# One softmax to a piece of other products, and gate chunks moved between the pairs of heads

## The chip, the cores and the metric

The kernel runs on one core of one Trainium2 chip. The metric is the device time of one execution in microseconds (us), less being better. TensorE multiplies, VectorE (DVE) and ScalarE (ACT) work on elements, GpSimd (POOL) does little here, and SyncE (SP) issues the loads. Each engine takes its instructions in one fixed order, and an instruction that must wait holds up all behind it on its engine.

## The reference

The work is a trunk of two layers over 256 latent tokens with 256 context tokens ahead of them, 2048 wide. Cut to what matters:

```python
for l in range(2):
    shift, scale, gate = silu(c) @ w_mod[l] + b_mod[l]      # 6144 numbers, also for c_ctx in layer 0
    h = rmsnorm(x) * (1 + scale) + shift
    q, k, v, g_att, u_pool, g_pool, a, b, g_conv = split(h @ w_in[l])   # 6656 columns
    s = q @ k.T / 8                        # 8 heads, two scores per head
    p = softmax(s)
    o = (p[0] - lam * p[1]) @ v
    y_att = rmsnorm(o) * silu(g_att)
    y_pool = pool(u_pool) * silu(g_pool)
    y_conv = conv(a, b) * silu(g_conv)     # depthwise, width 31, then a product of 512 by 512
    x = x + gate * (concat(y_att, y_pool, y_conv) @ w_out[l])
out = rmsnorm(x)                           # latent tokens only
```

Latent queries see all 512 keys; context queries see the 256 context keys only, and only in layer 0. In layer 1 the context goes no further than its keys and values.

## The kernel before

**Products.** Every large product is made of three products of numbers split in two: high by high, low by high, high by low. A weight piece of 128 by 1024 numbers (512 KB) is loaded by SP, copied to its high part by ScalarE (L205) and subtracted to its low part by VectorE (L206). The input projection is cut in 26 chunks of 256 columns, each four pieces of 24 matmuls; the output projection in eight chunks, o0 to o6 and "last". In layer 0, and in the k and v chunks of layer 1, a matmul of a chunk has 512 columns (FULL); in the other chunks of layer 1 it has 256 (HALF).

**What stands between the pieces.** The order of the chunks is written out by hand (`ORDER`, `ORDER_1`). The names are q, k, v, the gates ga (attention), gp (pooling), gc (convolution), the pooling input u and the convolution inputs a, b, with the number of the pair of heads or half. After each piece `project` calls `pump` (L251) with a budget, 3.4 for a FULL piece and 0.8 for a HALF one. `pump` takes steps from four queues in turn: `context_work`, `urgent` (attention and pooling), `conv_work`, `mod_work`. A step is a generator's run up to its next `yield`, and the number that it yields is taken off the budget. What the urgent queue leaves of a budget goes to the convolution, and what that leaves to `mod_work`. The recorded instructions are then put in order by a scheduler with priorities, engine by engine; the order that came out is shown below with the change.

**Attention.** `attention` (L709) works through the jobs of one pair of heads: per head two blocks of latent queries ("x") and in layer 0 the context ("c"). A job's front is its scores (`sx`, `sc`, L660) and its softmax (maximum L634 and the weighted difference L649 on VectorE, exponentials L640 on ScalarE, result `ex`). Its back is the transposes of `ex` (`atx`, L684), their split (`ahx`, `alx`) and the value products (`ox`, `oc`, L701 to L703). The front of job j is recorded before the back of the job ahead of it. A chunk q empties the urgent queue before it is taken, and so does a chunk ga whose pair has no normaliser yet.

**Modulation.** The 6144 numbers per layer that `c` gives are made in units of 1024 columns by `mod_on_dve` (L347) for the part that first-stage code does not cover: units (0,4), (0,5), then (1,0) to (1,3), and later (1,4), (1,5). A unit has 16 raws of 512 KB (`mraw`, loaded at L356 in two buffers) and for each raw two products on VectorE (one for `c`, one for `c_ctx`), added up in `macc` (L370, L372), of which there is one buffer. Then TensorE transposes `macc` (`modt`, L383), ScalarE adds up (L387) and `finish_mod` (L290, L293) writes the numbers. They are needed at the start of the next layer, and two places see to that: the queue gets what the budgets leave, and at o5 of each layer what is left of it is recorded at once:

```python
                ps = project(yh, yl, (0, L.n), f"o{i}_{l}")
                if i == 5:
                    drain(mod_work)
```

**The boundary of the layers.** Behind o6 the chunk "last" of layer 0 is multiplied in four parts (`ps_last`, 48 matmuls of 256 columns each). From its latent half the normaliser of layer 1 (`rms_v`, `rms_rstd`) and then `h` of layer 1 are made, on which `ps_b`, the first chunk of layer 1, depends.

Of the kernel before, what the change touches and what calls it, by code (L numbers as in the profile page):

```python
# [34 lines left out]


ORDER = (
    "b0 a0 q0 k0 v0 u0 b1 a1 q1 k1 v1 q2 k2 v2 q3 k3 v3 u1 ga1 gc0 ga2 gp0 ga0 ga3 gp1 gc1"
).split()
ORDER_1 = (  # L40
    "b0 a0 q0 k0 v0 u0 b1 a1 q1 ga0 k1 v1 q2 k2 gc1 v2 q3 k3 v3 u1 ga1 ga3 gc0 ga2 gp1 gp0"
).split()
OFFSET = {"q": 0, "k": 1024, "v": 2048, "ga": 3072, "u": 4096, "gp": 4608, "a": 5120, "b": 5632, "gc": 6144}

# [7 lines left out]
MOD_TAGS = ("whi", "wlo", "mraw", "whi", "wlo", "mraw", "whi", "wlo")  # L52

FULL, HALF = 3.4, 0.8
FRONT_0 = 2.0
FRONT, BACK = 1.5, 0.7
WAIT_MOD = 4.0
WAIT_CONV = 3.0

# [10 lines left out]
def trunk(  # L70
# [30 lines left out]
    def tmp(name, dt=F32):  # L101
        return tp.tile([P, T], dt, tag="t", name=name)
# [4 lines left out]
    def bank(name):  # L107
        return tr.tile([P, T], F32, tag="tr", name=name)
# [33 lines left out]
    def rsqrt(v, n, name, a=None, y=None):  # L142

        if a is None:
            nc.gpsimd.tensor_tensor(out=v, in0=v, in1=half[:, 0:1].to_broadcast([P, n]), op=ALU.pow)
            return
        nc.vector.tensor_scalar(
            out=y.bitcast(I32), in0=v.bitcast(I32), scalar1=-0.5, scalar2=1597463007.0, op0=ALU.mult, op1=ALU.add
        )
        for step in range(3):  # L150
            nc.vector.tensor_mul(out=a, in0=y, in1=y)
            nc.vector.scalar_tensor_tensor(out=a, in0=a, scalar=-0.5, in1=v, op0=ALU.mult, op1=ALU.mult)
            nc.vector.scalar_tensor_tensor(out=v if step == 2 else y, in0=a, scalar=1.5, in1=y, op0=ALU.add, op1=ALU.mult)
# [469 lines left out]
    def take_v(L, p, ps):  # L623
        L.vh = at.tile([P, 4, WC], F32R, tag="vh", name=f"vh{L.l}_{p}")
        L.vl = at.tile([P, 4, WC], F32R, tag="vl", name=f"vl{L.l}_{p}")
        with tc.high_priority(offset=V_BY):
            split_act(L.vh, L.vl, ps.rearrange("p b (c n) -> p (b c) n", n=WC))
        urgent.append(attention(L, p))
# [33 lines left out]
    def attend_front(L, p, h, which, qt):  # L662

        name = f"{which}{L.l}_{2 * p + h}_{qt}"
        ps = mm.tile([P, 2, T], F32, tag="mm", name=f"s{name}")
        if which == "x":
            scores(L, ps, slice(0, T), h, slice(qt * P, (qt + 1) * P), slice(0, T))
        else:
            for q in range(2):
                scores(L, ps, slice(q * TL, (q + 1) * TL), h, slice(TL + q * P, TL + (q + 1) * P), slice(TL, T))  # L670
        return softmax(L, ps, T, 1, name) if which == "x" else softmax(L, ps, TL, 2, name)

    def attend_back(L, p, h, which, qt, a):
        head = 2 * p + h
        name = f"{which}{L.l}_{head}"
        if qt == 0:
            L.ah = at.tile([P, 4, TL], F32R, tag="ah", name=f"ah{name}")
            L.al = at.tile([P, 4, TL], F32R, tag="al", name=f"al{name}")
        ah, al = L.ah, L.al
        b = bank(f"at{name}_{qt}")  # L680
        if which == "x":
            k0, nk, ts, qs = 0, 4, slice(0, TL), slice(qt * P, (qt + 1) * P)
            for kt in range(4):
                nc.tensor.transpose(b[:, kt * P : (kt + 1) * P], a[:, kt * P : (kt + 1) * P], ident)  # L684
            split_act(ah[:, :, qs], al[:, :, qs], b.rearrange("p (k q) -> p k q", q=P))
            if qt == 0:
                return
        else:
            k0, nk, ts = 2, 2, slice(TL, T)
            bv = b.rearrange("p (k q) -> p k q", q=TL)  # L690
            for q in range(2):
                for kt in range(2):
                    nc.tensor.transpose(
                        bv[:, kt, q * P : (q + 1) * P], a[:, q * TL + kt * P : q * TL + (kt + 1) * P], ident
                    )
            split_act(ah[:, :2, :], al[:, :2, :], bv)
        o = bank(f"o{name}")
        hs = slice(h * P, (h + 1) * P)
        for i in range(nk):
            kt = k0 + i  # L700
            nc.tensor.matmul(o[:, :TL], lhsT=L.vh[:, kt, hs], rhs=ah[:, i, :], start=i == 0, stop=False)  # L701
            nc.tensor.matmul(o[:, :TL], lhsT=L.vh[:, kt, hs], rhs=al[:, i, :], start=False, stop=False)
            nc.tensor.matmul(o[:, :TL], lhsT=L.vl[:, kt, hs], rhs=ah[:, i, :], start=False, stop=i == nk - 1)  # L703
        nc.scalar.copy(out=L.y[head][:, ts], in_=o[:, :TL])
        if which == "x":
            L.osq[h] = tmp(f"osq{name}")
        nc.scalar.activation(L.osq[h][:, ts], o[:, :TL], AF.Square)

    def attention(L, p):  # L709
        l, n = L.l, L.n  # L710
        L.osq = [None, None]
        jobs = []
        for h in range(2):
            jobs += [(h, "x", 0), (h, "x", 1)] + ([(h, "c", 0)] if L.ctx else [])
        prev = None
        for j in jobs:
            a = attend_front(L, p, *j)
            yield FRONT if prev else FRONT_0
            if prev:
                attend_back(L, p, *prev)  # L720
                yield BACK
            prev = j + (a,)
        attend_back(L, p, *prev)
        yield BACK

        nh = n // 2
        b = bank(f"ssq{l}_{p}")[:, :nh]
        for h in range(2):
            for half in range(2):
                c = 32 * (2 * h + half)  # L730
                nc.tensor.matmul(
                    b[c : c + 32, :], lhsT=ones[:, 0:32], rhs=L.osq[h][:, half * nh : (half + 1) * nh],
                    start=True, stop=True, skip_group_check=True,
                )
        v = one.tile([P, TL], F32, tag=f"arv{p}", name=f"arv{l}_{p}")[:, :nh]
        nc.vector.tensor_scalar(out=v, in0=b, scalar1=1.0 / P, scalar2=EPS, op0=ALU.mult, op1=ALU.add)
        work = tmp(f"arw{l}_{p}")
        rsqrt(v, nh, f"ars{l}_{p}", work[:, :nh], work[:, TL : TL + nh])
        L.arstd[p] = v
        yield 4.0  # L740
# [488 lines left out]
```

## Time and profile before

| what | value |
|---|---|
| median of 3 runs | 1495.96 us (1493.52 to 1496.93) |
| the profiled execution, its own time | 1502.84 us |
| its span, first to last instruction | 1501.0 us |
| TensorE busy | 1452.5 us (97%) |
| VectorE busy | 1112.8 us (74%) |
| ScalarE busy | 650.2 us (43%) |
| mean granted clock of TensorE | 0.992 |

The profiled execution lies 6.9 us above the median of the other runs, and 1.84 us of its time lie outside its span. Positions below are in us from the span's start. The stages, by the names of what TensorE writes: layer 0's attention chunks from 185 to 612, its other gates to 752, o0 to o5 to about 885, the boundary to 938, layer 1's attention from 1019 to 1365, the end 1501. A clock of 1.00 is TensorE's full granted speed, 2.4 GHz, and 0.5 the lower level of 1.2 GHz.

### The profile page before, as it was taken

Reading aid. Unit: us, or ns where it says so; the run is one execution under the profiler, and the core shown is the slowest. Engines: PE = TensorE matmul, PEld = TensorE weight load, DVE = VectorE, ACT = ScalarE, POOL = GpSimd, SP = SyncE. Lnnn points to the kernel's source line nnn. Section 1 sums busy time; section 2 is a strip of 40 time slices with the busy share of each in tenths; the row PEclk is TensorE's granted clock in tenths of the full one; section 3 lists DMA queues with packets and bytes.
Section 4 is the critical chain, followed back from the end, with each engine's and each line's share of the span. In section 5 each row is a group of like instructions: output and inputs, shape, how many; then the busy total and the mean of one; then the engine's idle time right before and its main releaser. Section 6 shows DMA issues by size and latency. Waiting matters only on the chain.

```text
span 1501.0 us, 23277 instructions
## 1 busy us (share of the span) xinstructions
PE 1452.5 (97%) x9196; PEld 1241.8 (83%) x9196; DVE 1112.8 (74%) x1641; ACT 650.2 (43%) x1245; POOL 9.0 (1%) x46
## 2 busy tenths in 40 slices
PE   4999999999999999999999999999999999999997
PEld 3567977897797977888888889988989897999997
DVE  4446999997549865879898964998995567475655
ACT  4224363227546363332433242635545545464543
POOL 0000000000000000000000000000000000000000
PEclk9999999999999999999999999999999999999998
DMA  8995226432234613655667761436733264245553
GB/s 332 397 391 221 81 88 202 148 110 74 74 112 146 202 60 113 221 195 203 209 213 250 243 222 55 142 114 216 265 113 124 79 227 161 99 134 178 187 183 113
DMA packets 75855, 258.90 MB, mean 172 GB/s; under 512 B 8800, under 2 KB 11104, under 8 KB 75744
## 3 DMA queue, kind: packets, MB, share of 16 engines
q1 hardware_dynamic: 75456, 257.14, 49.2%
q8 instruction: 72, 1.18, 0.3%
q14 instruction: 39, 0.32, 0.1%
q10 hardware_dynamic: 288, 0.26, 0.1%
HBM read 255.27 MB, written 2.10 MB: 171 GB/s over the span
## 4 chain that ended last, share of the span: by engine, by line
PE 83%; DVE 7%; DMA 4%; issue 3%; ACT 2%; SPq 0%; POOL 0%; POOLq 0%; DVEq 0%; ACTq 0%
PE ps_o L236 16%; PE ps_k L236 12%; PE ps_ga L236 9%; PE ps_v L227 7%; PE ps_q L236 6%; PE ps_gc L236 5%; PE ps_gp L236 4%; PE ps_first L236 4%; PE ps_b L236 3%; PE ps_u L236 3%; PE ps_a L236 3%; DMA mraw<-in_w_mod 3%; PE modacc L336 2%; DVE s L479 2%; DVE macc L372 1%
## 5 line engine op out<-in xcount | busy, mean ns | idle before, releaser
L372 DVE SCALAR_TENSOR_TENSOR macc<-mraw,c_sb,macc 128x1024 f32<-128x1024 f32 x210 | 262.6, 1280 | 32.2 <-DMA mraw<-in_w_mod 31.5
L236 PE MATMUL ps_o<-yh,out_h 128*128 128x512 f32 (+1 forms) x448 | 151.7, 339 | 0.0
L236 PE MATMUL ps_o<-yl,out_h 128*128 128x512 f32 (+1 forms) x448 | 151.6, 338 | 0.0
L236 PE MATMUL ps_o<-yh,out_l 128*128 128x512 f32 (+1 forms) x448 | 151.6, 338 | 0.0
L227 PE MATMUL ps_v<-in_v_h,hh 128*128 128x256 f32 x512 | 145.2, 284 | 0.0
L227 PE MATMUL ps_v<-in_v_h,hl 128*128 128x256 f32 x512 | 144.8, 283 | 0.0
L227 PE MATMUL ps_v<-in_v_l,hh 128*128 128x256 f32 x512 | 144.3, 282 | 0.0
L479 DVE SCALAR_TENSOR_TENSOR s<-cu,vec,s 128x512 f32<-128x512 f32 (+1 forms) x240 | 136.5, 615 | 0.5
L205 ACT CAST out_h<-out_r 128x1024 fp32r<-128x1024 f32 x56 | 58.8, 1050 | 111.5 <-PE ps_o L236 97.2
L236 PE MATMUL ps_k<-hh,in_k_h 128*128 128x512 f32 x256 | 102.9, 402 | 1.9 <-ACT ex L640 1.0
L236 PE MATMUL ps_k<-hl,in_k_h 128*128 128x512 f32 x256 | 102.1, 399 | 0.0
L236 PE MATMUL ps_k<-hh,in_k_l 128*128 128x512 f32 x256 | 101.8, 398 | 0.0
L227 PEld LDWEIGHTS ps_v<-in_v_l,hh 128*128 128x128 f32 x512 | 96.7, 189 | 0.3
L227 PEld LDWEIGHTS ps_v<-in_v_h,hh 128*128 128x128 f32 x512 | 96.7, 189 | 0.3
L227 PEld LDWEIGHTS ps_v<-in_v_h,hl 128*128 128x128 f32 x512 | 96.4, 188 | 0.0
L236 PEld LDWEIGHTS ps_o<-yl,out_h 128*128 128x128 f32 x448 | 84.3, 188 | 9.9
L236 PEld LDWEIGHTS ps_o<-yh,out_h 128*128 128x128 f32 x448 | 84.3, 188 | 9.9
L236 PEld LDWEIGHTS ps_o<-yh,out_l 128*128 128x128 f32 x448 | 84.3, 188 | 9.8
L206 DVE TENSOR_TENSOR out_l<-out_r,out_h 128x1024 fp32r<-128x1024 f32 x56 | 68.1, 1223 | 32.1 <-ACT out_h L205 30.7
L236 PE MATMUL ps_ga<-hh,in_ga_h 128*128 128x512 f32 (+1 forms) x256 | 87.2, 340 | 1.0 <-ACT ex L640 1.0
L236 PE MATMUL ps_ga<-hl,in_ga_h 128*128 128x512 f32 (+1 forms) x256 | 87.0, 340 | 0.0
L236 PE MATMUL ps_ga<-hh,in_ga_l 128*128 128x512 f32 (+1 forms) x256 | 87.0, 340 | 0.0
(407 smaller groups left out, 3708.2 us busy)
## 6 DMA issues: line engine op xcount, KB each, us to landing
mraw<-in_w_mod SPq DMA_DIRECT2D x128, 512.0 KB, 4.3
wm<-in_w_mod SPq DMA_DIRECT2D x64, 512.0 KB, 8.5
out_r<-in_w_out SPq DMA_DIRECT2D x56, 512.0 KB, 4.0
in_k_r<-in_w_in SPq DMA_DIRECT2D x32, 512.0 KB, 4.4
in_v_r<-in_w_in SPq DMA_DIRECT2D x32, 512.0 KB, 3.4
in_ga_r<-in_w_in SPq DMA_DIRECT2D x32, 512.0 KB, 3.8
in_q_r<-in_w_in SPq DMA_DIRECT2D x28, 512.0 KB, 3.5
in_u_r<-in_w_in SPq DMA_DIRECT2D x16, 512.0 KB, 3.4
```

Source lines behind the costliest of these rows:

```text
L205: nc.scalar.copy(out=hi, in_=raw)
L206: nc.vector.tensor_sub(out=lo, in0=raw, in1=hi.bitcast(F32))
L227: nc.tensor.matmul(o, lhsT=a[:, ts], rhs=b[:, j, :], start=f and n == 0 and tt % 2 == 0, stop=e and n == 2, skip_group_check=True,)
L236: nc.tensor.matmul(ps[:, nt, t0:t1], lhsT=a[:, j, ns], rhs=b[:, t0:t1], start=f and n == 0, stop=e and n == 2,)
L336: nc.tensor.matmul(acc[c : c + 32, :n], lhsT=sc32[:, k, :], rhs=raw[:, j, :], start=k < 4, stop=k >= KT - 4, skip_group_check=True,)
L372: nc.vector.scalar_tensor_tensor(out=acc[:, r, :], in0=raw, scalar=sc[:, k, r : r + 1], in1=acc[:, r, :], op0=ALU.mult, op1=ALU.add)
L479: nc.vector.scalar_tensor_tensor(out=acc, in0=u[:, :nq, j : j + TL], scalar=w[:, j : j + 1], in1=acc, op0=ALU.mult, op1=ALU.add)
```

## The change

Three things are changed. First, `attention` yields once per job and no longer twice: the front of job j, then the back of the job ahead of it, then one yield of 3.4 (layer 0) or 2.4 (layer 1). So a FULL piece's budget of 3.4 takes one whole job in layer 0, where before it took a front of 1.5, a back of 0.7 and the next front. For a pair with six jobs in layer 0 that is seven steps that each use up a budget (six jobs and the last back with what follows), against four budgets before. Second, in `ORDER` ga0 and ga1 move up, from the end of the layer to between the pairs. Third, in `ORDER_1` ga0 moves from inside pair 1 to behind v1, gp0 from the end to behind it, and ga1 from behind u1 to between pair 2's and pair 3's chunks.

```diff
--- before.py
+++ after.py
@@ -35,10 +35,10 @@
 
 
 ORDER = (
-    "b0 a0 q0 k0 v0 u0 b1 a1 q1 k1 v1 q2 k2 v2 q3 k3 v3 u1 ga1 gc0 ga2 gp0 ga0 ga3 gp1 gc1"
+    "b0 a0 q0 k0 v0 u0 b1 a1 q1 k1 v1 ga0 q2 k2 v2 ga1 q3 k3 v3 u1 gc0 ga2 gp0 ga3 gp1 gc1"
 ).split()
 ORDER_1 = (
-    "b0 a0 q0 k0 v0 u0 b1 a1 q1 ga0 k1 v1 q2 k2 gc1 v2 q3 k3 v3 u1 ga1 ga3 gc0 ga2 gp1 gp0"
+    "b0 a0 q0 k0 v0 u0 b1 a1 q1 k1 v1 ga0 gp0 q2 k2 v2 gc1 ga1 q3 k3 v3 u1 ga2 gc0 ga3 gp1"
 ).split()
 OFFSET = {"q": 0, "k": 1024, "v": 2048, "ga": 3072, "u": 4096, "gp": 4608, "a": 5120, "b": 5632, "gc": 6144}
 
@@ -52,8 +52,7 @@
 MOD_TAGS = ("whi", "wlo", "mraw", "whi", "wlo", "mraw", "whi", "wlo")
 
 FULL, HALF = 3.4, 0.8
-FRONT_0 = 2.0
-FRONT, BACK = 1.5, 0.7
+ATTEND, BACK = (3.4, 2.4), 0.7
 WAIT_MOD = 4.0
 WAIT_CONV = 3.0
 
@@ -715,10 +714,9 @@
         prev = None
         for j in jobs:
             a = attend_front(L, p, *j)
-            yield FRONT if prev else FRONT_0
             if prev:
                 attend_back(L, p, *prev)
-                yield BACK
+            yield ATTEND[l]
             prev = j + (a,)
         attend_back(L, p, *prev)
         yield BACK
```

Three places show how the instructions move. The names in a row are output<-inputs, with the scheduler's buffer numbers at the end; the number before them is the line.

**VectorE at the boundary of the layers.** The unit in question is unit 3 of layer 1 (`macc1_3`, raws `mraw1_3_0` to `_15`). Before, from `out0_6_0_l` on, VectorE has only splits of weights and residuals `s` here:

```order
L206 TENSOR_TENSOR out0_6_0_l_7621<-out0_6_0_r_7618,out0_6_0_h_7620 128x1024
L290 TENSOR_TENSOR mod1_119<-modsum1_3_7545,vec1_85 128x16
L293 SCALAR_TENSOR_TENSOR mod1_119<-mod1_119,vec1_85 128x16
L206 TENSOR_TENSOR last0_0_1ql_7794<-last0_0_r_7791,last0_0_0qh_7793 128x1024
L206 TENSOR_TENSOR out0_6_1_l_7666<-out0_6_1_r_7663,out0_6_1_h_7665 128x1024
L206 TENSOR_TENSOR last0_1_1kl_7800<-last0_1_r_7797,last0_1_0kh_7799 128x1024
L807 SCALAR_TENSOR_TENSOR s10_y_3676<-ps_o5_0_7482,mod0_118,xr5_0_7478 128x256 x2
L807 SCALAR_TENSOR_TENSOR s11_y_3677<-ps_o5_0_7482,mod0_118,xr5_1_7479 128x256 x2
L206 TENSOR_TENSOR out0_6_3_l_7696<-out0_6_3_r_7693,out0_6_3_h_7695 128x1024
L1075 TENSOR_TENSOR sq_acc_120<-sq_acc_120,nsq0_10_7650 128x512
L206 TENSOR_TENSOR last0_3_1vl_7806<-last0_3_r_7803,last0_3_0vh_7805 128x1024
L1075 TENSOR_TENSOR sq_acc_120<-sq_acc_120,nsq0_11_7655 128x512
```

Of the change, the rows from the eleventh raw of unit 3 on (line numbers are one or two lower than before):

```order
L371 SCALAR_TENSOR_TENSOR macc1_3_7514<-mraw1_3_10_7579,c_sb_83,macc1_3_7514 128x1024 x2
L371 SCALAR_TENSOR_TENSOR macc1_3_7514<-mraw1_3_11_7583,c_sb_83,macc1_3_7514 128x1024 x2
L205 TENSOR_TENSOR last0_1_1kl_7800<-last0_1_r_7797,last0_1_0kh_7799 128x1024
L371 SCALAR_TENSOR_TENSOR macc1_3_7514<-mraw1_3_12_7587,c_sb_83,macc1_3_7514 128x1024 x2
L371 SCALAR_TENSOR_TENSOR macc1_3_7514<-mraw1_3_13_7591,c_sb_83,macc1_3_7514 128x1024 x2
L805 SCALAR_TENSOR_TENSOR s12_103<-ps_o6_0_7662,mod0_118,xr6_0_7658 128x256 x2
L805 SCALAR_TENSOR_TENSOR s13_104<-ps_o6_0_7662,mod0_118,xr6_1_7659 128x256
L371 SCALAR_TENSOR_TENSOR macc1_3_7514<-mraw1_3_14_7595,c_sb_83,macc1_3_7514 128x1024 x2
L371 SCALAR_TENSOR_TENSOR macc1_3_7514<-mraw1_3_15_7599,c_sb_83,macc1_3_7514 128x1024 x2
L805 SCALAR_TENSOR_TENSOR s13_104<-ps_o6_0_7662,mod0_118,xr6_1_7659 128x256
L205 TENSOR_TENSOR last0_3_1vl_7806<-last0_3_r_7803,last0_3_0vh_7805 128x1024
L205 TENSOR_TENSOR last0_2_1al_7812<-last0_2_r_7809,last0_2_0ah_7811 128x1024
```

All 32 products of unit 3 now stand between `out0_6_0_l` and `last0_3_1vl`, with the splits of out0_6_1, out0_6_3, out0_6_2 and last0_1 among them and those of last0_3 and last0_2 behind the last product. Before, the last of these products stood ahead of `out0_5_3_l`. What came before in the layer is shifted by a unit: `macc1_0` starts behind the split of in0_ga3 where it started behind that of in0_ga2.

**TensorE at unit 3's transposes.** Before, `modt1_3` stands within o5:

```order
L236 MATMUL ps_o5_0_7482<-yh0_7_6619,out0_5_1_l_7486 128x512
L383 MATMUL modt1_3_0_7546<-ident_82,macc1_3_7109 128x128 x4
L383 MATMUL modt1_3_2_7556<-ident_82,macc1_3_7109 128x128 x4
L236 MATMUL ps_o5_0_7482<-yh0_12_6623,out0_5_3_h_7517 128x512
L236 MATMUL ps_o5_0_7482<-yl0_12_6624,out0_5_3_h_7517 128x512
L236 MATMUL ps_o5_0_7482<-yh0_12_6623,out0_5_3_l_7518 128x512
L236 MATMUL ps_o5_0_7482<-yh0_12_6623,out0_5_3_h_7517 128x512
L236 MATMUL ps_o5_0_7482<-yl0_12_6624,out0_5_3_h_7517 128x512
L383 MATMUL modt1_3_4_7566<-ident_82,macc1_3_7109 128x128 x4
```

Of the change it stands within the first half of "last":

```order
L235 MATMUL ps_last0_0_1_7864<-yh0_12_6516,last0_3_0vh_7805 128x256
L235 MATMUL ps_last0_0_1_7864<-yl0_12_6517,last0_3_0vh_7805 128x256
L382 MATMUL modt1_3_0_7606<-ident_82,macc1_3_7514 128x128
L382 MATMUL modt1_3_2_7616<-ident_82,macc1_3_7514 128x128
L382 MATMUL modt1_3_0_7606<-ident_82,macc1_3_7514 128x128 x3
L382 MATMUL modt1_3_2_7616<-ident_82,macc1_3_7514 128x128 x3
L235 MATMUL ps_last0_1_0_7937<-yh0_0_6478,last0_0_0qh_7793 128x256
L235 MATMUL ps_last0_1_0_7937<-yl0_0_6479,last0_0_0qh_7793 128x256
L235 MATMUL ps_last0_0_0_7815<-yh0_12_6516,last0_3_1vl_7806 128x256
L382 MATMUL modt1_3_4_7626<-ident_82,macc1_3_7514 128x128 x4
```

So `modt1_3`, which needs the last product into `macc1_3`, moved from o5 to the middle of "last". Where `modt1_3` stood in o5 there is now `modt1_2`. Between the end of `modt1_2` and the first row of `modt1_3` TensorE has 137 matmuls of o5 and o6 and 52 of "last"; 140 of the 192 of "last" stand behind it.

**TensorE at the first softmaxes of layer 0.** Before, `sx0_0_0` and `sx0_0_1` stand side by side, then come the 24 matmuls of a piece of u0, and then:

```order
L236 MATMUL ps_u0_0_1788<-hh0_7_135,in0_u0_1_l_1792 128x512
L660 MATMUL sc0_0_0_1894<-kh0_0_1528,qh0_0_1362 128x256 x2
L660 MATMUL sc0_0_0_1894<-kl0_0_1529,qh0_0_1362 128x256 x2
L660 MATMUL sc0_0_0_1894<-kh0_0_1528,ql0_0_1363 128x256 x2
L660 MATMUL sc0_0_0_1894<-kh0_0_1528,qh0_0_1362 128x256 x2
L684 MATMUL atx0_0_0_1887<-ident_82,ex0_0_0_1828 128x128 x4
L660 MATMUL sc0_0_0_1894<-kl0_0_1529,qh0_0_1362 128x256 x2
L660 MATMUL sc0_0_0_1894<-kh0_0_1528,ql0_0_1363 128x256 x2
L660 MATMUL sx0_1_0_1945<-kh0_0_1528,qh0_0_1362 128x512 x2
```

Of the change, a piece of u0 stands between `sx0_0_0` and `sx0_0_1`, and the transposes come two matmuls behind the latter:

```order
L235 MATMUL ps_u0_0_1788<-hh0_7_135,in0_u0_1_l_1792 128x512
L659 MATMUL sx0_0_1_1867<-kh0_0_1528,qh0_0_1362 128x512 x2
L659 MATMUL sx0_0_1_1867<-kl0_0_1529,qh0_0_1362 128x512 x2
L659 MATMUL sx0_0_1_1867<-kh0_0_1528,ql0_0_1363 128x512 x2
L235 MATMUL ps_u0_0_1788<-hh0_12_145,in0_u0_3_h_1839 128x512
L235 MATMUL ps_u0_0_1788<-hl0_12_146,in0_u0_3_h_1839 128x512
L683 MATMUL atx0_0_0_1887<-ident_82,ex0_0_0_1828 128x128 x4
L235 MATMUL ps_u0_0_1788<-hh0_12_145,in0_u0_3_l_1840 128x512
L235 MATMUL ps_u0_0_1788<-hh0_12_145,in0_u0_3_h_1839 128x512
```

From the end of `sx0_0_0` to `atx0_0_0` TensorE now has 24 matmuls of u0, three rows of scores and two matmuls of u0; before it had the three rows of `sx0_0_1`, the 24 matmuls and four rows of `sc0_0_0`.

## Rows read from the trace of the kernel before

**Rows 1.** The page, first part: engine, busy us, share of the span, instructions.
```profile
PE 1452.5 (97%) x9196; PEld 1241.8 (83%) x9196; DVE 1112.8 (74%) x1641; ACT 650.2 (43%) x1245; POOL 9.0 (1%) x46
```

**Rows 2.** Busy time by stage (--windows), all engines, with granted clock.
```profile
752.00:877.00 125.00, 125.00 (x545) 100.70 (x544) 113.11 (x119) 35.92 (x69) 0.00 (x0) 1.00 0.71 238
877.00:938.00 61.00, 60.55 (x371) 53.41 (x370) 27.94 (x48) 22.38 (x57) 1.16 (x7) 1.00 0.34 115
```

**Rows 3.** The same view, TensorE alone, first part of the boundary of the layers.
```profile
877.00:912.60 35.60, 35.60 (x162) 1.00 0.53 181
```

**Rows 4.** The same view, instructions that touch macc alone, on two stretches.
```profile
752.00:877.00 125.00, 2.35 (x16) 1.92 (x17) 71.15 (x58) 1.00 0.71 238
877.00:938.00 61.00, 2.35 (x16) 1.63 (x15) 0.00 (x0) 1.00 0.34 115
```

**Rows 5.** Chain of waits at the boundary: start, length, what.
```profile
877.21 0.87 PE modt L383 x8
...
880.88 31.84 PE ps_o L236 x137
...
912.75 1.23 DVE s L807 x3
...
926.23 0.70 POOL rms_v L145
...
926.98 0.71 PE rms_rstd L160 x4
927.69 9.84 PE ps_last L236 x83
937.53 7.47 PE ps_b L236 x63
```

**Rows 6.** VectorE's timeline before and at the boundary: start, length, what.
```profile
858.15 4.86 DVE L372 SCALAR_TENSOR_TENSOR macc<-mraw,c_sb,macc 128x1024 f32<-128x1024 f32 x4
...
882.26 0.17 DVE L290 TENSOR_TENSOR mod<-modsum,vec 128x16 f32<-128x16 f32 x1 [2.90 <-ACT modj L387]
```

**Rows 7.** Source view of L356 (the loads of raws), 800 to 880 us.
```profile
L356 SPq DMA_DIRECT2D mraw<-in_w_mod x18: 327/328/328, 800.7 to 872.6; - x18
...
DMA to landing us min/median/max: 3.4/4.4/4.7
```

**Rows 8.** Waits of TensorE in layer 0's attention: us, times, longest.
```profile
PE atx L684 <- DVE ex L649: 2.3, 3, 1.6
PE oc L701 <- ACT ahc L212: 1.1, 2, 0.6
...
PE ox L701 <- DVE alx L213: 0.7, 1, 0.7
```

**Rows 9.** A lone softmax of layer 1 on VectorE's timeline.
```profile
1307.08 1.23 DVE L206 TENSOR_TENSOR in_u_l<-in_u_r,in_u_h 128x1024 fp32r<-128x1024 f32 x1 [0.41 <-ACT in_u_h L205]
...
1312.51 0.75 DVE L649 SCALAR_TENSOR_TENSOR ex<-ex,rx 128x512 f32<-128x512 f32 x1
```

**Rows 10.** TensorE's timeline, the end of the scores of that softmax.
```profile
1306.89 0.39 PE L236 MATMUL ps_u<-hh,in_u_h 128*128 128x256 f32 x1
```

**Rows 11.** Waits of TensorE in layer 1's attention.
```profile
PE atx L684 <- DVE ex L649: 6.2, 2, 3.6
PE ps_k L236 <- ACT ex L640: 1.0, 1, 1.0
PE ps_ga L236 <- ACT ex L640: 1.0, 1, 1.0
```

**Rows 12.** Busy time and granted clock around the two longest of these waits.
```profile
1030.00:1039.00 9.00, 6.44 (x39) 5.69 (x39) 8.76 (x14) 5.55 (x12) 0.00 (x0) 0.81 0.70 221
...
1247.00:1250.80 3.80, 3.80 (x15) 2.05 (x13) 3.09 (x5) 3.53 (x8) 0.00 (x0) 0.52 0.60 215
1250.80:1258.20 7.40, 7.40 (x35) 6.34 (x35) 6.32 (x9) 3.24 (x9) 0.00 (x0) 0.79 0.53 155
```

**Rows 13.** VectorE's timeline, a product that waits for its raw in layer 1.
```profile
1231.69 1.28 DVE L372 SCALAR_TENSOR_TENSOR macc<-mraw,c_sb,macc 128x1024 f32<-128x1024 f32 x1 [0.94 <-DMA mraw<-in_w_mod]
```

## The prediction

> **What bounds the kernel now.** I read the page's first part, then the busy time by stage, and only then the waits, because the share of TensorE says where anything can be won at all. TensorE is busy for 1452.5 us of a span of 1501.0, VectorE for 1112.8 [rows 1], so the kernel is a queue of matmuls, and a change of order can only win what TensorE now waits, or lose by making it wait. At the output projection there is nothing to win: from 752 to 877 TensorE is busy all the time, while VectorE works 113.1 of 125 us [rows 2], 71.2 of them on the products into `macc` [rows 4]. At the boundary of the layers, 877 to 938, VectorE has only 27.9 us of work in 61 [rows 2] and none of it is `macc` [rows 4], since the last unit of layer 1's numbers was finished in o5; TensorE runs without a gap from 877 to 912.6 [rows 3], and behind it the chain goes on through "last" to `ps_b`, the first chunk of layer 1, at 937.53 [rows 5]. So there is slack on VectorE in one place, and the change puts something into it.
>
> **What can be won.** In layer 0's attention TensorE waits 2.3 us for `ex`, 1.1 for `ahc` and 0.7 for `alx`, 4.1 in all [rows 8]. In layer 1's attention it waits 6.2 us for `ex` in two waits and twice 1.0 for the exponentials, 8.2 in all [rows 11]. Behind a long wait the granted clock falls: 0.52 for 3.8 us and 0.79 for 7.4 us after the wait of 3.6, 0.81 in the stretch of 9 us with the wait of 2.6 [rows 12]. A clock of 0.5 is the lower of the two levels, so 0.52 means 3.6 us at the lower level, 0.79 some 3.1 us and 0.81 some 3.4 us; half of each is lost: 1.8 + 1.55 + 1.7 = 5.1 us. All that the change could win is therefore 4.1 + 8.2 + 5.1 = 17.4 us.
>
> **Term 1, the boundary.** A pair of layer 0 takes seven budgets where it took four, so less reaches `mod_work`, and the units of layer 1's numbers run late. The order shows by how much: unit 2's transposes stand where unit 3's stood in o5, and all 32 products of unit 3 come behind them. There is one `macc` buffer, so the first product waits for the end of unit 2's transposes, which I put where unit 3's end now, at 880.88 [rows 5].
>
> The work of VectorE from there to the last product: four products take 4.86 [rows 6], 1.2 each; 30 at 1.2 and the first two of a unit, which are plain products, at some 0.7 (an estimate) make 37.5. Among them stand five splits of weights (last0_0, out0_6_1, out0_6_3, out0_6_2, last0_1) at 1.15 (the 1.23 of [rows 9] less the overlap of neighbours), 5.7; seven residuals at 1.23/3 = 0.41 [rows 5], 2.9; and `finish_mod`, two of 0.17 [rows 6], 0.3. Sum 46.4: with every raw there in time the last product would end at 927.3.
>
> The raws are not there in time. A load is issued when its buffer is free, that is after the second product of the raw two before it, and lands a median 4.4 us later (3.4 to 4.7) [rows 7]. Two products take 2.4. A raw thus comes round every 6.8 us in each of two buffers, and two raws are used per round: 882.4 (first raw done) + 7 x 6.8 + 2.4 = 932.4. The splits and residuals lie inside the waits. I take 932.4, the later of the two limits.
>
> TensorE's work until it needs the last product: 137 matmuls take 31.84 [rows 5], then 52 of 256 columns at 9.84/83 = 0.119 [rows 5], 6.2. Together 38.0: it is done at 918.9 and waits 13.5 us for `modt1_3`, in one piece or partly ahead of o6's late splits. Two splits of "last" stand behind the last product, so it goes on at about 934. Then come 0.9 for the transposes [rows 5], 140 matmuls at 0.12, 16.8, and some 1.7 for the chain of the normaliser (0.70 and 0.71 in [rows 5], and a residual); `ps_b` starts at about 953.4 instead of 937.5, **+16**. A wait of this length has a lower clock behind it; the like of rows 12 would be 1.5 to 3.4 us, but the wait may come in several pieces. I add 1: **+17**. Bounds: with landings hidden +11 with the clock, with 4.7 instead of 4.4 seven rounds add 2.1, with the full price of the clock 2.4 more, +22.
>
> The Trainium skill ("Trainium Kernel Development and Optimization", Best Practices) says that double buffering overlaps loads with compute. By that rule the two buffers of raws hide the loads and the boundary costs +11 in place of +17; the trace disagrees so far, since a landing of 4.4 [rows 7] is longer than the 2.4 of products that cover it, and VectorE waits 0.94 for such a raw in layer 1 [rows 13].
>
> **Term 2, layer 0's attention.** The distance between a softmax's scores and its transposes hardly changes: 24 x 0.232 + scores 0.85 + two matmuls 0.5 = 7.0 us. A lone softmax in layer 1 takes from 1306.89, when its scores are done [rows 10], to 1313.25, 6.4 us with one split in its way [rows 9]. So it fits by 0.6, and the back-to-back scores that now make VectorE do two maxima in a row are gone. A product into `macc` (1.2) on top would cost 0.6. Some of the waits should go: I take -2.5, between -4.1 (all) and +5 (some eight softmaxes of the last pair with 0.6 each, because `macc` now stands densely there).
>
> **Term 3, layer 1's attention.** The order of pair 0 is the same, so its wait of 2.6 stays. Pair 2's backs move from a chunk of k (pieces of 24 x 0.232 = 5.6 us) under ga1 (24 x 0.119 = 2.9). There VectorE has four splits (4.8), five products into `macc` (6.0) with waits for raws of some 0.8 (an estimate by the 0.94 of [rows 13]), 4, and some 10.9 of softmax and gate work, 25.7, while TensorE has 20.3: up to +5.4 new. The other pairs have 19 of VectorE under 24 of TensorE. Against that stand the second wait of 3.6 and the two of 1.0, which may go. I take +1.5, between -13.3 (all waits and the clock) and +7.
>
> The gates' moves cost nothing by themselves: the same matmuls, splits and loads, hidden under TensorE as before; if the cover is gone it is what term 3 says. Loads on SP move with their chunks; raws of unit 3 stand among those of "last" and of layer 1's first chunk, which by the sum are needed later than they land.
>
> **Sum.** 17 - 2.5 + 1.5 = +16 on the span of 1501.0: 1517. The profiled execution took 1502.84, 1.84 beyond its span, and lies 6.9 above the median of the runs, 1495.96; I carry the +16 over to the median: **1512**.
>
> **The rivals.**
>
> *A: the waits of the attention go, and that outweighs the boundary.* For it: scores are now spread out, one maximum at a time, and most waits are for `ex`. With all 17.4 won and +11 to +17 lost at the boundary the time is 1489.5 to 1496; it decides as soon as the boundary costs less than the attention wins. Against it: pair 0 of layer 1 keeps its order, and with it 2.6 us and its 1.7 of clock, so 13.1 are the most that I see. Chance 0.14, split into 0.09 faster and 0.05 the same; time 1494.
>
> *B: the double buffer hides the raws.* Then the boundary is bound by VectorE's 46.4 us: +11, and the sum is +10, 1506. For it: the shortest landing of 3.4, and the splits and residuals among the products, which give the loads more time. Against it: the median of 4.4. Chance 0.22.
>
> *C: ga1 and the pairs of layer 1 become bound by VectorE, and the loads of raws land late.* +7 in place of +1.5 and +22 in place of +17: +26.5, 1522. For it: waits for raws in layer 1 [rows 13]. Against it: mean work of VectorE stays below TensorE's. Chance 0.12.
>
> The Trainium skill ("TensorE: Matmul & The Clock Gate", HAM oscillation) says that gaps in TensorE's work bring the clock down, so one gap costs more than its length. The traces agree at 0.52 behind the 3.6 us [rows 12]; by it the boundary could cost up to 2.4 more than I take.
>
> **How the numbers follow.** My forecast, +13 to +20, has 0.52. The range of eight in ten leaves out rival A and the far half of C: **1500 to 1521**. About 0.2% (3 us) is what a measurement of this kernel can tell from no change. Faster by more than that 0.09 (A), within it 0.07 (A's rest and the low end of B), slower 0.84.
>
> **What would show it.** Right: in 880 to 950 of the changed profile TensorE idles 8 to 15 us with `macc` or a raw as the releaser, VectorE's `macc` work there is about 38 us where it was none, the raws' landing is the releaser of `macc` in every round, `ps_b` of layer 1 starts about 13 to 16 us later than before, a lower clock shows behind the gap; up to o5 the time lies 2 to 3 us ahead of before. Rival B: `macc` runs without gaps. Rival A: no wait for `ex` left in either layer. The prediction is wrong if TensorE's idle time at the boundary is under 5 us, for instance because loads land faster there or because o6's splits come in time, or if a wait in the attention grows instead of shrinking.

## The result

The changed kernel takes 1513.78 us (median, 1510.26 to 1514.44, 4 runs) against 1496.45 of the kernel before beside it (1493.52 to 1498.2, 4 runs). The ratio is 1.0113, with a 95% interval of 1.0094 to 1.0133, so 14 to 20 us slower. The forecast was 1512.

**The profile after.** The page's first part of the changed kernel, as in [rows 1]:

```profile
PE 1457.2 (96%) x9196; PEld 1241.4 (82%) x9196; DVE 1115.5 (74%) x1641; ACT 662.8 (44%) x1253; POOL 8.9 (1%) x46
```

The span is 1512.2 us. VectorE's work is the same within 3 us, and TensorE's within 5, so it is not more work but work at another place. Busy time by stage (all engines, then granted clock, share of the DMA engines and GB/s), the stretches that answer to [rows 2]; the boundary now ends at 953, not at 938:

```profile
752.00:877.00 125.00, 125.00 (x550) 101.01 (x548) 111.78 (x116) 36.04 (x77) 0.00 (x0) 1.00 0.71 236
877.00:953.00 76.00, 65.11 (x380) 56.88 (x380) 65.50 (x84) 24.88 (x83) 1.17 (x7) 0.93 0.59 198
```

The same view for the instructions that touch `macc`, answering to [rows 4]:

```profile
752.00:877.00 125.00, 3.38 (x24) 2.72 (x24) 70.92 (x58) 1.00 0.71 236
877.00:953.00 76.00, 5.71 (x24) 3.79 (x24) 38.30 (x32) 0.93 0.59 198
```

Up to 877 nothing has changed: 70.9 us of VectorE on `macc` where there were 71.2, and TensorE busy all the time. Behind it stand 32 products, 38.3 us, where there were none. The chain of waits at the boundary (start, length, what), answering to [rows 5]:

```profile
750.33 55.77 PE ps_o L235 x240
...
878.20 0.57 PE modt L382 x4
...
886.33 4.73 DMA mraw<-in_w_mod
...
902.37 4.32 DMA mraw<-in_w_mod
...
920.12 4.19 DMA mraw<-in_w_mod
...
927.99 1.29 DVE macc L371
929.33 1.54 PE modt L382 x6
...
951.77 8.90 PE ps_b L235 x75
```

The reader is to see that the chain, which before ran along TensorE's own rows, now runs from a raw's transfer (three steps of 4.2 to 4.7 us are shown) to products into `macc`, to the last product at 927.99 to 929.3, and over the transposes of unit 3 back to TensorE. `ps_b` of layer 1 starts at 951.77 instead of 937.53 [rows 5], though o0 starts 1.9 us earlier, at 750.33.

The chain's steps through loads are longer than what the loads cost, because VectorE does splits and residuals while a raw is under way. VectorE alone from unit 3's first product to its last, and then from the source view of the loads (L355, 870 to 930 us) who waited for them and how long they took to land:

```profile
878.80:929.28 50.48, 46.66 (x47) 0.96 0.68 226
...
  DVE macc L371: 3.5, 5
...
DMA to landing us min/median/max: 3.3/3.9/4.7
```

It works 46.7 of the 50.5 us and idles 3.5 for raws, five times. TensorE's waits at the boundary (us in all, times, longest):

```profile
PE modt L382 <- DVE macc L371: 8.8, 2, 8.3
PE ps_last L235 <- DVE last_1kl L205: 0.9, 1, 0.9
PE ps_o L235 <- DVE out_l L205: 0.7, 1, 0.7
PE ps_last L235 <- DVE s_y L805: 0.5, 1, 0.5
```

and its clock (busy us, granted clock, share of the DMA engines, GB/s):

```profile
929.00:933.00 4.00, 3.67 (x16) 0.50 0.69 229
933.00:937.00 4.00, 4.00 (x29) 0.75 0.86 303
...
1260.00:1264.00 4.00, 4.00 (x15) 0.50 0.78 221
1264.00:1268.00 4.00, 4.00 (x28) 0.74 0.38 134
```

Behind the wait of 8.3 the clock is 0.50 for 4 us and 0.75 for the next 4, that is 2 + 1 = 3 us lost; the last two rows are the same fall in layer 1, behind a wait of 3.0. The waits of the attention, layer 0 as [rows 8] and then layer 1 as [rows 11]:

```profile
PE atx L683 <- DVE ex L648: 2.7, 1, 2.7
PE ox L701 <- DVE alx L212: 0.9, 5, 0.2
...
PE oc L700 <- ACT ahc L211: 0.4, 2, 0.2
```

```profile
PE atx L683 <- DVE ex L648: 6.0, 3, 3.0
```

In layer 0 the sum is what it was, 4.0 for 4.1, but 2.7 of it are now in one wait, where the longest was 1.6 [rows 8]. Behind that wait the clock falls, which it does nowhere in layer 0's attention before (busy us, granted clock, share of the DMA engines, GB/s):

```profile
583.00:587.00 4.00, 4.00 (x14) 0.57 0.69 218
```

That is 1.7 us lost. In layer 1 the waits are 6.0 for 8.2, in three waits instead of four.

### The profile page after: what moved, and what is told of

Read it like the earlier page. It is cut to its first block, busy times and chain, and to the rows that moved or that the text cites. A ratio compares the mean times of both kernels' runs of the same rounds, so it can differ in the third digit from the quotient of the medians.

```text
span 1512.2 us, 23250 instructions
## 1 busy us (share of the span) xinstructions
PE 1457.2 (96%) x9196; PEld 1241.4 (82%) x9196; DVE 1115.5 (74%) x1641; ACT 662.8 (44%) x1253; POOL 8.9 (1%) x46
## 4 chain that ended last, share of the span: by engine, by line
PE 82%; DVE 7%; DMA 6%; ACT 3%; issue 2%; SPq 0%; POOL 0%; DVEq 0%; POOLq 0%; ACTq 0%
PE ps_o L235 13%; PE ps_k L235 11%; PE ps_ga L235 9%; PE ps_v L226 8%; PE ps_q L235 7%; PE ps_first L235 4%; DMA mraw<-in_w_mod 4%; PE ps_gp L235 4%; PE ps_gc L235 4%; DVE macc L371 3%; PE ps_u L235 3%; PE ps_b L235 3%; PE ps_a L235 3%; PE modacc L335 2%; PE sx L659 1%
```

## The experiments

Two changes of the kernel, yields and chunk orders, act on two layers, so I undid them one at a time, then took the late unit itself away. For the comparison I read three lengths off TensorE's timeline in each run: from the first matmul of k0 to the first of o0 in layer 0, from there to layer 1's first chunk (the boundary with the output projection ahead of it), and from there to layer 1's o0. Single executions, in us, good to about 0.1; the medians of the kernel before in the four batches are 1496.4 to 1497.4, and each ratio is to its own batch:

| kernel | median | ratio to before, interval | k0 to o0 | o0 to layer 1 | layer 1 to its o0 |
|---|---|---|---|---|---|
| before | 1496.45 | | 612.2 | 185.4 | 460.7 |
| the change | 1513.78 | 1.0113 [1.0094, 1.0133] | 611.6 | 201.4 | 458.9 |
| e1, old yields | 1503.32 | 1.0038 [1.0025, 1.0051] | 614.6 | 185.5 | 459.1 |
| e2, old orders | 1511.33 | 1.0083 [1.0058, 1.0107] | 619.2 | 193.4 | 454.9 |
| e3, layer 1's part alone | 1500.03 | 1.0012 [0.9999, 1.0025] | 612.1 | 185.4 | 460.5 |
| e4, layer 0's part alone | 1511.04 | 1.0084 [1.0061, 1.0108] | 609.7 | 201.8 | 453.4 |
| e5, e4 with budget 4.6 | 1513.47 | 1.0104 [1.0084, 1.0123] | 618.2 | 196.1 | 455.7 |
| e6, e4 with budget 5.8 | 1534.63 | 1.0251 [1.0228, 1.0274] | 641.9 | 194.6 | 453.5 |
| e7, unit 3 cut to two raws | 1501.71 | 1.0032 [1.0018, 1.0046] | 612.3 | 188.4 | 458.9 |
| e8, three buffers of raws | 1525.3 (one run) | | 608.4 | 213.3 | 460.8 |
| e9, e5 with three buffers | 1503.7 | 1.0041 [1.0025, 1.0057] | 599.8 | 205.4 | 456.7 |
| e10, before with three buffers | 1496.0 | 0.9992 [0.9977, 1.0007] | 611.5 | 185.5 | 454.1 |
| e11, layer 1's yields alone | 1496.52 | 0.9993 [0.9979, 1.0007] | 612.0 | 185.4 | 453.7 |

In e9 the scheduler set the first matmuls of o0 among the last gate chunk, so there only the sum of two columns means something: 805.2, against 814.3 in e5, 836.5 in e6, 797.6 before and 811.5 in e4. The last column also shows that layer 1 of the kernel before, in the execution whose rows were shown, was 4 to 7 us longer than the same order and yields of layer 1 in e4, e5, e6, e9 and e10 (453.4 to 456.7). That is where most of that execution's 6.9 us above the median lay.

**e1, the new chunk orders with the old yields.** Edit against the changed kernel (the constants are left out):

```diff
-            if prev:
-                attend_back(L, p, *prev)
-            yield ATTEND[l]
+            yield FRONT if prev else FRONT_0
+            if prev:
+                attend_back(L, p, *prev)
+                yield BACK
```

> The changed chunk orders with the yields of before (front and back apart). In its order unit 3 of layer 1's numbers ends in o5 again, as before the change. Theory (the late unit at the boundary of the layers costs 16 us and the rest next to nothing): 1494 to 1499, no macc at the boundary and TensorE busy there. Rival (the gates between the pairs, that is the chunk orders, make the loss): 1508 to 1514 with new waits in the attention.

1503.32, between the two theories: the boundary is back at 185.5, 16 us shorter than in the change, so the late unit makes that part. But layer 0 is 3 us longer than in the change, and 6 us above the kernel before remain. TensorE waits in layer 0 up to o0:

```profile
PE atx L684 <- DVE ex L649: 5.0, 4, 2.0
```

5.0 us for `ex`, where before it was 2.3 [rows 8], and layer 1 takes 459.1 instead of 454. By these single executions the chunk orders with gates between the pairs cost some 2.4 in layer 0 and 5 in layer 1 by themselves.

**e2, the new yields with the old orders.** Edit against the kernel before:

```diff
-            yield FRONT if prev else FRONT_0
             if prev:
                 attend_back(L, p, *prev)
-                yield BACK
+            yield ATTEND[l]
```

> The new yield (one softmax to a piece) with the chunk orders of before. In its order unit 3 starts in o4's last piece and ends within the boundary, some 28 us earlier than in the changed kernel. Theory (late unit): the last product is done about 28 us earlier, by about 905, before TensorE needs it, so the boundary costs 0 to 3 and the time is 1495 to 1500. Rival (the new yields themselves lose in the attention): 1508 to 1514.

1511.33, a miss for the theory and within the rival's range. The first half of it: in layer 0 the new yields with the old orders lose 7 us. Waits that were not there (up to o0):

```profile
PE ps_k L235 <- ACT ex L639: 3.4, 2, 1.7
PE atx L683 <- DVE ex L648: 1.9, 1, 1.9
PE oc L701 <- DVE alc L212: 1.9, 2, 0.9
```

All waits there are 8.1 us where they were 5.2, so they alone are not the 7. Twice a wait of 0.9 and one of 1.7 stand close together, and there the granted clock is low (TensorE's busy us, clock, share of the DMA engines, GB/s):

```profile
372.00:379.00 7.00, 5.93 (x18) 0.52 0.01 2
474.00:481.50 7.50, 5.82 (x22) 0.55 0.00 0
```

That is 3.4 us lost each time, 6.7 in all, while some 2 us of transposes are gone from here to the boundary: most of the 7 is the clock. The second half is the boundary. Unit 3 did start earlier, but the chain shows that it was slower than I took it:

```profile
855.78 0.57 PE modt L382 x4
...
895.01 3.87 DMA last_r<-in_w_out
...
907.82 3.77 DVE macc L371 x3
```

It starts at the end of unit 2's transposes, 856.4, some 22 us earlier than in the change and not 28, and ends at 911.6, 55 us later where the change takes 50: among the products stand splits and residuals, and once one that waits for a weight's landing (895.01, 3.87). `modt` stands earlier on TensorE too, in o6, and waits there (2.3 us), and the boundary is 8 us longer than before. The rival is right for 7 us, the late unit for 8.

**e3 and e4, each layer's part alone.** e3 has the change's `ORDER_1` and yield 2.4 in layer 1 alone, e4 its `ORDER` and yield 3.4 in layer 0 alone; the edit is the diff above with a condition on `l`:

```diff
-            yield FRONT if prev else FRONT_0
+            if l == 0:
+                yield FRONT if prev else FRONT_0
...
+            if l == 1:
+                yield ATTEND
```

> Layer 0 as before, layer 1's order and yields of the change. Theory (late unit, which is layer 0's doing): 1493 to 1498, boundary as before at about 937. Rival (layer 1's chunks of 256 columns become bound by VectorE): 1503 to 1512, waits in layer 1 longer than the 6.0 us of the change.

> Layer 0's order and yields of the change, layer 1 as before; the late unit is as in the change. Theory (late unit): all of the loss, 1511 to 1516, ps_b of layer 1 starts at about 952. Rival (layer 1 makes half of the loss or more): 1500 to 1505.

e4 keeps the late unit and all but 3 us of the loss (1511.04), with a boundary of 201.8. e3 takes 1500.03, 2.7 above its own kernel before: between the theories, and the interval (0.9999 to 1.0025) does not exclude no change. It is about what e4 lacks to the whole (2.7 between the medians, 3.6 when each is held against its own batch). In the third length, single executions, layer 1 takes 460.5 where the old order takes 453.4 to 456.7 in all but one.

**e11, layer 1's yields without its order.** Against the kernel before; the old yields are kept for layer 0:

```diff
+            if l == 1:
+                yield ATTEND
```

> The kernel before with layer 1's yield of the change alone (2.4 once per softmax), all chunk orders as before. Theory (layer 1's loss of some 3 us comes from the gates between its pairs, whose pieces of 2.9 us stand where pieces of 5.6 stood): 1494 to 1498, no loss. Rival (the yield makes it): 1499 to 1502, as with the whole of layer 1's part.

1496.52, no loss, so the yields of layer 1 cost nothing that can be measured. The loss goes with the order: all five runs with the new `ORDER_1` take 458.9 to 460.8 in the last column, seven of the eight with the old one 453.4 to 456.7 (the eighth is the kernel before). Which of the moved chunks makes it is not shown. TensorE's waits for `ex` in layer 1, e3 and then e11:

```profile
PE atx L685 <- DVE ex L650: 6.0, 3, 2.6
```

```profile
PE atx L685 <- DVE ex L650: 4.6, 4, 2.2
```

The waits of e11 are four of at most 2.2, and no fall of the clock follows; those of e3 are three of up to 2.6, behind two of which the clock falls (0.57 over 4 us, then 0.72 and 0.50 over twice 4), and in the changed kernel the one of 3.0 at 1258 is followed by the 0.50 and 0.74 shown above. Of the 6.8 us between e3 and e11 in layer 1, 5.1 are this lower clock.

**e7, unit 3 with two raws for sixteen.**

```diff
+        pieces = [x for x in pieces if x[:2] != (1, 3) or x[3] in (0, KT - 1)]
```

> The changed kernel, in which unit 3 of layer 1's numbers adds up two of its 16 raws only (14 loads and 28 products left out). Theory (late unit): the boundary falls from 201.4 to about 186 and the time to 1496 to 1499; what is left over before is layer 1's. Rival (the boundary is long for another reason, as the splits of o6 and last that stand late): 1506 to 1514.

This kernel leaves out 14 loads and 28 products of unit 3. The time falls to 1501.71, 3 us above the theory's range and far below the rival's, and the boundary to 188.4, TensorE running almost without a gap (busy us, clock):

```profile
877.00:940.00 63.00, 61.66 (x377) 1.00 0.37 122
```

The splits of o6 and "last", and everything else, are where the change has them. So 13 of the 16 us at the boundary are the 28 products and 14 loads; some 2 of the other 3 are unit 3's 16 transposes (0.57 for four in the chain above), which now stand behind o0 with a third unit where there were two. What is left of the time, 4.9 us, is about layer 1's loss and those 3.

**e8, three buffers for raws** (and three for the other weights, to make room):

```diff
-MRAW = 2
+MRAW = 3
-        raw = wp.tile([P, 1024], F32, tag="raw", name=f"{name}_r", bufs=4)
+        raw = wp.tile([P, 1024], F32, tag="raw", name=f"{name}_r", bufs=3)
```

> The changed kernel with three buffers for raws and three instead of four for the other weights. The order puts all 32 products of unit 3 in one row ahead of the other splits of o6. Theory (a raw's landing of 4.4 behind a freed buffer sets the pace with two buffers): with three the products run at 1.2 without waits, some 38 us in a row, TensorE then waits for o6's second split till about 920 and the time is some 8 above the change, 1520 to 1524. Rival (the pace is what the transfers give, whatever the buffers): the row takes 54 us or more and the time is 1535 to 1545.

1525.3, one run, 1.3 above the theory's range. VectorE's timeline (start, length, what) has the products in one piece:

```profile
880.35 33.58 DVE L371 SCALAR_TENSOR_TENSOR macc<-mraw,c_sb,macc 128x1024 f32<-128x1024 f32 x28
```

28 products in 33.58, 1.20 each, without a wait: with a third buffer the raws are there in time. With two buffers the same 28 took from 883.8 to 929.3 in the change, 45.5 us: some 34 of products, 3.5 of waiting for raws, and the rest splits and residuals among them. Here the order puts the products all ahead of o6's next splits, and the unit's transposes ahead of o6's next matmuls, so TensorE stands still meanwhile:

```profile
PE modt L382 <- DVE macc L371: 21.2, 2, 20.7
```

So the third buffer takes the waits for raws away, but in the change these were 3.5 of the unit's 50.5 us and the rest VectorE's own work; and to make the unit faster does not help where the order lets it go first.

**e5 and e6, more of the units ahead of the output projection.** Layer 0's part alone, with a larger budget behind the pieces of the last six gate chunks:

```diff
-            pump(FULL if toks[1] - toks[0] == T else HALF)
+            pump((GATE if name in GATE_CHUNKS else FULL) if toks[1] - toks[0] == T else HALF)
```

> Layer 0's part of the change alone, with a larger budget (4.6 for 3.4, four products for three) behind the pieces of the last six gate chunks of layer 0, so that unit 3 ends at the first piece of o6. Theory (late unit): the boundary is short again, 185 to 188 us from o0 to layer 1's first chunk, and the time 1493 to 1498, since layer 0's attention has some 2.5 us to give. Rival (two raws come every 6.8 us and four products to a piece of 5.6 us hold up the splits behind them): the six gate chunks lengthen by up to 1.2 us per piece, 24 pieces, and the time is 1505 to 1525.

> The same with a budget of 5.8, five products to a piece; unit 3 ends in o4. Theory (late unit): boundary 185 us, 1493 to 1498. Rival (products that wait for raws hold up the splits): gate chunks longer than in the run with 4.6, 1505 to 1530.

The rival was right in both: e5, 1513.47, lies in its range and is no better than e4, and e6, 1534.63, lies 5 us above its range. Waits of TensorE from the gate chunks to the boundary, first with 4.6, then with 5.8:

```profile
PE modt L386 <- DVE macc L375: 3.4, 2, 2.7
PE ps_ga L239 <- DVE in_ga_l L209: 2.5, 1, 2.5
PE modt L386 <- ACT modj L390: 2.4, 1, 2.4
```

```profile
PE ps_ga L239 <- DVE in_ga_l L209: 8.8, 2, 7.0
PE modt L386 <- DVE macc L375: 6.0, 2, 5.5
PE ps_o L239 <- DVE out_l L209: 5.6, 1, 5.6
PE ps_gp L239 <- DVE in_gp_l L209: 4.4, 3, 2.1
```

The unit is no longer late, but the splits that stand behind the extra products are, and so are the transposes of the units before (in e5 in o0, in e6 in gc1).

**e9 and e10, the same with three buffers, and the control.**

> As the run with the budget of 4.6 (layer 0's part of the change alone), with three buffers for raws and three for the other weights. Theory (with two buffers a raw's landing held up the products and the splits behind them): the gate chunks and o0 to o5 take what they took before the change, the boundary about 185, and the time is 1493 to 1498. Rival (four products and a split, 5.95 us of VectorE, are more than a piece of 5.57 in any case): 1503 to 1512.

> The kernel before with the same buffers, three for raws and three for the other weights, as the control for the run beside it. Theory (nothing waits for raws where TensorE would feel it, save in layer 1's pair 2): the same within 0.2%, or up to 4 us faster by layer 1's waits. Rival (the fourth weight buffer is needed in chunks of 256 columns): 1500 to 1510.

The control stands at 1496.0, no change. e9 takes 1503.7, 9.8 less than e5: with raws there in time the waits of splits are nearly gone, and what is left is again a unit's transposes that wait for its last product, now between gc1 and o0:

```profile
PE modt L386 <- DVE macc L375: 3.3, 2, 2.7
PE ps_o L239 <- DVE yl L216: 0.9, 1, 0.9
```

It is the theory's way and the rival's size. No run beat the kernel before by more than can be measured, so there was no better version to run.

## Why the prediction was right

**Term 1, the boundary: right in mechanism and nearly in size.** Predicted +17, measured 201.4 - 185.4 = 16.0. The last product was to end at 932.4, or 930.3 with the 2 us by which the change arrived earlier; it ended at 929.3. e7 takes the unit away and 13 us go. Of the two limits that were worked out for the last product, VectorE's own work (46.4) came out at 46.7; the landings (51.5 for the whole unit) added 3.5 us of idle time and not the 5.1 between the limits, since raws landed in a median 3.9 and not 4.4, and they were the releaser before five of the raws and not in every round. The parts for TensorE were less good than the sum, which had 13.5 of waiting and 1.6 of late splits behind it, 0.9 for unit 3's transposes and 1 for the clock. TensorE waited 8.8 for `modt` and 2.1 for late splits and residuals, 10.9 in all and 10.4 more than before: the unit was 1 us shorter, TensorE's own work meanwhile some 39 us and not 38 (878.8 to 919.7 less the 2.1), and its first transposes need only the first of the last two products. The transposes cost some 2, and the lower clock 3 (near the full price that I had as a bound). 10.4 + 2 + 3 is 15.4 of the 16.0. The waits were put too high by 4.7 and the other two too low by 3; that these nearly cancel is luck. The lower bound has a slip: with landings hidden the sum is 10.9 without the clock and 11.9 with it.

**Term 2, layer 0's attention: no gain to speak of.** Predicted -2.5, measured -0.6 in the change and -2.5 in e4, of which some 2 are the transposes that went to the boundary. The waits moved and their sum stayed (4.0 for 4.1): that most of them should go was wrong, and one grew, from 1.6 at the longest to 2.7, which the prediction had named as a sign of being wrong; for this term it was. The 1.7 of clock behind that wait are most of the 1.9 between the change and e4, where the wait at the same place is 2.4 and the clock stays full. e1 and e2 show, in single executions, that the new orders alone cost 2.4 there and the new yields alone 7, most of it clock; together they undo each other.

**Term 3, layer 1: right sign, mis-sized.** Predicted +1.5; e3 gives 2.7 by the medians (at the edge of what can be told) and 4 to 7 by the lengths. The step that failed is the place: I had the four splits and five products under ga1 as the worst, with up to 5.4 of new wait, and the second long wait as likely to go. It stayed, at gc1 (3.0 with the fall of the clock). e11 and the last column of the table show that the order costs this and not the yield; that it is the gates under the softmaxes is the likely reason and not shown by itself.

**The sum** of +16 stands against 17.3 between the medians, by 16.0 at the boundary, about -1 in layer 0 and +2.7 in layer 1. I had carried it from a profiled execution that was 6.9 above the median; its surplus lay in layer 1's two waits and their clock, so to subtract "all waits and the clock", 13.3 us, as the most that term 3 could win was too generous: e4, with the same layer 1, has 2.2 us less of these waits and none of the lower clock.

**The rivals.** A, that the attention's waits go and outweigh the boundary: they did not go. B, that two buffers hide the raws: nearer than I took it, for they hid all but 3.5 us, but the boundary cost 16 and not 11; with three buffers the waits are gone (e8). Best Practices in the Trainium skill ("Trainium Kernel Development and Optimization") asks for double buffering to overlap loads with compute; in this trace two buffers overlapped all but those 3.5 us. C, layer 1 bound by VectorE and late raws: its direction in layer 1, a third of its size.

## What to carry to other kernels

A queue of background work that is drained at a fixed point hides its cost until the budgets ahead of it shrink: look at where its last unit lands in the order of every engine, since a delay of one unit shows only where the drain is, here some 300 us later than the first softmaxes that it moves. Changes that alter how many budgets a step takes are to be costed by what the lowest queue gets. And where background products wait for their own loads, larger budgets move that wait into the splits ahead of the matmuls (e5, e6); a third buffer took back 9.8 us of it (e9), though not all.

## What was not expected

The kernel before has two waits in layer 1 that are not the same in another execution of the same layer 1. In the rows shown they were 6.2 us together, 2.6 and 3.6, and the clock behind them 0.81, 0.52 and 0.79 [rows 11, 12]. In e4, with the same code in layer 1, they are

```profile
PE atx L685 <- DVE ex L650: 4.0, 2, 2.2
```

and the clock behind them is full (the second one; busy us, granted clock, share of the DMA engines, GB/s):

```profile
1255.00:1260.00 5.00, 3.80 (x21) 1.00 0.79 263
```

2.2 us more of waits and the 5.1 of clock that the prediction worked out make 7.3, the whole difference of layer 1 between the two executions (460.7 and 453.4). Layer 0 of e4 is not the kernel before's, so what makes the waits differ is not shown.

"TensorE: Matmul & The Clock Gate" in the Trainium skill, on HAM oscillation, says that gaps bring the clock down. The rows here agree in so far as each fall at the boundary and in the attention stands at a wait. But the length of the wait does not settle it. In layer 1 of e7 a wait of 2.5 us has the full clock behind it, and in layer 1 of e2 one of 1.8 has 0.57 (the wait, then TensorE's busy time and clock behind it; e7, then e2):

```profile
PE atx L684 <- DVE ex L649: 2.5, 1, 2.5
...
1036.50:1040.50 4.00, 4.00 (x31) 1.00 0.55 194
```

```profile
PE atx L683 <- DVE ex L648: 1.8, 1, 1.8
...
1256.00:1260.00 4.00, 3.71 (x15) 0.57 0.80 237
```

So a wait of some 2 us may cost its own length or 1.7 us more, and differences of a few us between single executions are to be read with the clock beside them.
